# A hybrid decoder block on one core: the modulation's shifts summed by VectorE instead of TensorE

## The chip, the cores and the metric

The kernel runs on one core of one Trainium2 chip. The metric is device microseconds of that core for one execution. The engines are named as the profile names them: PE is TensorE (PEld its weight loads), DVE is VectorE, ACT is ScalarE, POOL is GpSimd, SP is SyncE, which here issues nearly all transfers.

## The reference

One block of width 2048 over a sequence of 256 tokens, in float32. What matters here is the modulation: a conditioning vector `c` of 2048 numbers gives six vectors that shift, scale and gate the two sub-layers.

```python
mod = jax.nn.silu(c) @ w_mod[l] + b_mod[l]            # w_mod: 2048 x (6 * 2048)
sh1, sc1, g1, sh2, sc2, g2 = jnp.split(mod, 6, axis=-1)
h = rms_norm(x, norm1_g[l]) * (1.0 + sc1[:, None]) + sh1[:, None]
proj = h @ w_in[l]                                     # q, k, v, u, gates
...                                                    # attention; S5 scan on u; merge by gates; w_out
x = x + g1[:, None] * (merged @ w_out[l])
h2 = rms_norm(x, norm2_g[l]) * (1.0 + sc2[:, None]) + sh2[:, None]
...                                                    # h2 @ w_up, depthwise conv, gating, w_down
x = x + g2[:, None] * (ffn)
```

Each of the six parts is a product of one row with a 2048 x 2048 matrix: 16 MB of weights that are read once and used once.

## The kernel before

**Weights.** Every matrix comes from HBM in tiles of 128 x 1024 float32 (512 KB), issued by SP one after the other in the order of one list, `plan`. A tile of a dense product is split in two for accuracy: ACT copies it to `whi` (line 186), DVE takes the difference `wlo` (line 191), and PE multiplies both parts. There are five raw tiles in the ring `raw`, two of `whi` and two of `wlo`; the split of a step is issued one step ahead of its matmuls (`split_ahead`). A raw tile is free for the next transfer when its last reader is done. A fourth-stage pool (`post`) adds a second ring of four tiles, `mraw`, for the modulation alone, from the GLU product on.

**Modulation.** Tiles of the modulation are put between the weight steps at a given rate per step (`with_mods`); PE, DVE and ACT meet them in that order.
- The scales and shifts (parts 1, 0, 4, 3) go through `mod_block` (line 443): PE multiplies silu(c), laid out in columns (`cpad`), with the raw tile in four column groups of the array, 128 to 512 columns at a time. A block covers 2 or 4 groups of 128 output channels. When its tiles are through, ACT copies the row sums to SBUF (`rows`, line 463) and `cols_of` (line 475) turns them to columns: PE transposes, one DVE reduction, one addition.
- The gates (parts 2 and 5) go through `gate_block` (line 482): their weights are stored transposed, so that a tile holds half of the inputs of 128 output channels, and one DVE instruction (line 493) multiplies it with silu(c), held on all partitions in `cb`, and sums along the row. `cb` is made by `silu_rows` (line 503) when the `post` pool opens: a transfer of `c` to 128 partitions on POOL's queue (line 505) and one ACT instruction (line 506).

**Stages.** (1) `xT` is loaded, squares are summed for the first norm, and the modulation of the first two channel groups is made. (2) The product with `w_in` runs over the input channels in five chunks (`CHUNKS`, 2, 2, 4, 4, 4 groups of 128): while PE works on a chunk, the scale and then the shift of the next chunk pass by (`mod1`, line 579), and at their end `make_h` modulates the next chunk's `h`. In the last chunk the first quarter of sh2 and sc2 passes (`mod2`, line 1078). The generator `setup` (line 599), which makes the tables of the rotary embedding and of the scan mostly on DVE, runs in the background of these chunks, a piece per 1/0.9 steps; it starts when the scale of the second chunk is there (`place["a1"]`). (3) The rest of the gate products (`gsp`), then `gap` and `pap`: attention and the S5 scan run in the background of these, and the quarters 1 to 3 of sc2 and sh2 pass by at 1.3 tiles a step, but for the last four units (`LATE`), which come after the second norm. (4) `glup`, `ppp` and `outp`, with the tiles of g1 among them, then the second norm. (5) The FFN with the tiles of g2.

**The scan** (`ssm_scan`, line 749) handles eight channel tiles in turn. `prepare` builds the matrices of one tile and ends in the matmuls `bu` (line 815), whose result DVE rotates (lines 852 to 857) and scans (line 862); `leave` multiplies the states out (line 830) and `finish` adds the skip term. Its steps are spread by `yield`, 1.05 to a weight step. `prepare` of the next tile comes before `leave` of the present one, with two buffers of `cpad` and `blocks`, and the tag `s4` has three buffers.

**Queues.** The order of an engine's instructions isn't that of the program text: the build moves an instruction ahead when its inputs are ready and others wait. Within an engine they then run strictly in order, and a waiting one holds up all behind it.

Of the kernel before, what the change touches and what calls it, by code (L numbers as in the profile page):

```python
# [42 lines left out]
def block_kernel(ctx: ExitStack, tc: tile.TileContext, I, out):  # L43
# [54 lines left out]
    LATE = 4  # L98
# [294 lines left out]
    A.activation(cpad[:, :, 0], p0[:, 0:16], AF.Silu)  # L393

    def rsqrt(y, v, t):
        V.tensor_scalar(y.bitcast(I32), v.bitcast(I32), -0.5, 1597463007.0, op0=ALU.mult, op1=ALU.add)
        for _ in range(3):
            V.scalar_tensor_tensor(t, y, -0.5, y, op0=ALU.mult, op1=ALU.mult)
            V.tensor_mul(t, t, v)
            V.scalar_tensor_tensor(y, t, 1.5, y, op0=ALU.add, op1=ALU.mult)  # L400
# [80 lines left out]

    def gate_block(part, k0, nk, cb, dst):

        st = {}
        base = 16 * (part // 5)

        def step(k, half, raw):
            flat = raw.rearrange("p a b -> p (a b)")
            if k == 0 and half == 0:
                st["s"] = sm.tile([128, nk, 2], F32, name="gsum", tag="gsum")  # L490
                V.tensor_copy(st["s"].rearrange("p a b -> p (a b)"), rb[:, 0:2 * nk])
            sums = st["s"]
            V.scalar_tensor_tensor(flat, flat, 1.0, cb[:, 1024 * half:1024 * half + 1024], op0=ALU.mult,  # L493
                                   op1=ALU.mult, accum_out=sums[:, k, half:half + 1])
            if k == nk - 1 and half == 1:
                ks = slice(k0, k0 + nk)
                V.tensor_add(dst[:, ks], sums[:, :, 0], sums[:, :, 1])
                V.tensor_add(dst[:, ks], dst[:, ks], b_mod[:, 16 * part + k0:16 * part + k0 + nk])

        return [[(I["w_g"][base + k0 + k, half], lambda raw, k=k, half=half: step(k, half, raw))]  # L500
                for k in range(nk) for half in range(2)]

    def silu_rows(pool):
        cb = pool.tile([128, 2048], F32, name="cb")
        G.dma_start(cb, I["c"].to_broadcast([128, 2048]))
        A.activation(cb, cb, AF.Silu)
        return cb

# [70 lines left out]
    def mod1(k0, nk):  # L579
# [8 lines left out]

        return mod_block(1, k0, nk, sc, m1_tile) + mod_block(0, k0, nk, sh, bu_tile)

# [5 lines left out]
    def s4(name, shape=(128, 2, 2, 256)):  # L596
        return sp.tile(list(shape), F32, name=name, tag="s4", bufs=3)

    def setup():

        def hold(elem):

            V.tensor_copy(elem, a1[:, place["a1"]:place["a1"] + 1])
# [13 lines left out]
        cs = [take(2, 64) for i in range(2)]  # L617
        bt = s4("bt", (128, 2, 16, 32))
        hold(bt[:, 0, 0, 0:1])
        G.dma_start(bt, I["ssm_b"])  # L620
        yield 1
        while place["a1"] == 0:
# [110 lines left out]
        crb = cre[:, None, :].to_broadcast([128, 16, 32])  # L733
        cib = cim[:, None, :].to_broadcast([128, 16, 32])
        bb = sp.tile([128, 2, 16, 32], F32, name="z_b")
        b2 = s4("b2", (128, 16, 32))
# [12 lines left out]
    def ssm_scan(u):  # L749
# [6 lines left out]
        bpad = sp.tile([128, 2, 2, 4, 2, 16], F32, name="bpad")  # L756
        cpad = [sp.tile([128, 2, 3, 4, 2, 16], F32, name=f"cpad{i}") for i in range(2)]
        blocks = [sp.tile([128, 2, 128], F32, name=f"blocks{i}") for i in range(2)]
        zt = [sp.tile([128, 2, 2, 128], F32, name=f"zt{i}") for i in range(2)]
        dec = sp.tile([128, 2, 4, 64], F32, name="dec")  # L760
        for z in (bpad, *cpad, *blocks, *zt, dec):
            G.memset(z, 0.0)
# [4 lines left out]
        def prepare(ct):  # L767

            tt = slice(4 * ct, 4 * ct + 4)
            cp, kb = cpad[ct % 2], blocks[ct % 2]  # L770
            for g, gs in enumerate(halves):
# [46 lines left out]
        def leave(ct, w):  # L818
            cp, kb = cpad[ct % 2], blocks[ct % 2]
            st["py"] = y = py_tile([128, 2, 128], "py")  # L820
# [21 lines left out]
        for ct in range(8):  # L842
# [39 lines left out]
            yield 1  # L882
            if ct < 7:
                yield from prepare(ct + 1)
            leave(ct, w)
            yield 1
            yield 1
            finish(ct)


# [187 lines left out]
    def mod2(j):  # L1078
        lag = int(j < 3)

        def sc(rows):
            cols_of(rows, 4, 4 * j, 4, a2)
            scale_cols(a2, norm2_g, 4 * j, 4)

        return (mod_block(4, 4 * j, 4, sc, m1_tile, lag)
                + mod_block(3, 4 * j, 4, lambda rows: cols_of(rows, 3, 4 * j, 4, sh2),
                            m1_tile if j < 3 else bu_tile, lag))

# [48 lines left out]
    late = mods[len(mods) - LATE:]  # L1137
    del mods[len(mods) - LATE:]

# [45 lines left out]
    gt = [pair(c + 4, "yg") for c in range(4)]  # L1185
    cb = silu_rows(post)

# [7 lines left out]
    rest, mods[:] = list(mods), []  # L1195
    parts = [m for j in range(4) for m in gate_block(2, 4 * j, 4, cb, g1)]
    while parts or rest:
# [65 lines left out]
    for j in range(4):  # L1263
        mods += gate_block(5, 4 * j, 4, cb, g2)

# [76 lines left out]
def arrange(inputs):  # L1342
# [19 lines left out]
    for n in ("ssm_c_re", "ssm_c_im"):  # L1362
# [6 lines left out]
        "w_m": np.concatenate(w_m),  # L1369
        "w_g": np.concatenate([w_mod[:, 2].T, w_mod[:, 5].T]).reshape(32, 128, 2, 1024).swapaxes(1, 2),  # L1370
        "p0": pack([cols(a["c"]), cols(a["norm1_g"]), cols(a["norm2_g"]), cols(a["b_mod"]), np.eye(128)]),
# [37 lines left out]
```

## Time and profile before

| | |
|---|---|
| time, median of 3 runs (lowest to highest) | 1552.86 us (1548.08 to 1556.23) |
| time of the profiled execution | 1551.37 us |
| its span, first to last instruction | 1549.6 us |
| PE busy | 1491.3 us, 96% |
| PE weight loads busy | 1239.2 us, 80% |
| DVE busy | 1052.7 us, 68% |
| ACT busy | 847.4 us, 55% |
| transfers | 354.54 MB, mean 229 GB/s |
| mean granted TensorE clock | 0.992 of full speed |

The busy time of an engine is the union of its instructions. Matmuls overlap in the pipeline and their ends are modelled, so the cost of a matmul is better read from the distance between the starts of two neighbours than from its own length. A matmul with float32 operands stands in the profile as two records.

### The profile page before, as it was taken

What the parts mean: (1) busy time and instruction counts of PE and PEld (TensorE: products, weight loads), DVE (VectorE), ACT (ScalarE), POOL (GpSimd) and SP (SyncE); (2) the same over time, 40 slices, a digit from 0 to 9 for tenths busy, and PEclk for the clock granted to TensorE, in tenths of its full rate; (3) what the DMA queues carried; (4) which work ended last, traced back from release to release, by engine and by line L of the source; (5) the groups of instructions that cost most, each with busy time, mean ns of one, the idle gap of its engine ahead of it and who ended that gap; (6) DMA issues with size and microseconds to landing.
All of it is one profiled execution on the core that took longest, in us unless ns stands there. A gap on an engine that the chain in (4) does not pass through costs nothing.

```text
span 1549.6 us, 24718 instructions
## 1 busy us (share of the span) xinstructions
PE 1491.3 (96%) x9624; PEld 1239.2 (80%) x9624; DVE 1052.7 (68%) x1778; ACT 847.4 (55%) x1201; POOL 11.3 (1%) x25
## 2 busy tenths in 40 slices
PE   6999989999999999899989999999999999999998
PEld 3656757689886678788869888888888888888887
DVE  2787443786774567799769888887555576666654
ACT  3766656967674543654435555555444455555442
POOL 1000000000000000000000000000000000000000
PEclk9999999999999999999999999999999999999999
DMA  8887777643348776879877777776555555565663
GB/s 308 282 311 279 251 269 255 233 166 121 124 150 284 276 251 209 294 255 345 309 254 241 247 247 257 243 252 207 190 191 190 190 187 190 191 189 189 203 210 111
DMA packets 99252, 354.54 MB, mean 229 GB/s; under 512 B 10976, under 2 KB 13152, under 8 KB 99008
## 3 DMA queue, kind: packets, MB, share of 16 engines
q1 hardware_dynamic: 97808, 348.17, 65.5%
q0 software_dynamic: 1184, 4.66, 0.8%
q8 instruction: 75, 1.23, 0.3%
q14 instruction: 41, 0.34, 0.1%
q10 hardware_dynamic: 144, 0.14, 0.0%
HBM read 350.83 MB, written 2.10 MB: 228 GB/s over the span
## 4 chain that ended last, share of the span: by engine, by line
PE 78%; DVE 8%; DMA 8%; ACT 5%; issue 2%; SPq 0%; ACTq 0%; DVEq 0%; POOLq 0%
PE vp L302 10%; PE dp L302 10%; PE gp L302 10%; PE dp L304 5%; PE vp L304 5%; PE gp L304 5%; DMA raw<-in_w_in_dram 3%; PE outp L302 3%; DVE wlo L191 3%; PE modp L456 3%; PE gap L302 3%; ACT whi L186 2%; PE ppp L302 2%; PE outp L304 2%; PE gap L304 2%
## 5 line engine op out<-in xcount | busy, mean ns | idle before, releaser
L191 DVE TENSOR_TENSOR wlo<-raw,whi 128x1024 fp32r<-128x1024 f32 x464 | 566.8, 1224 | 404.4 <-ACT whi L186 401.9
L186 ACT CAST whi<-raw 128x1024 fp32r<-128x1024 f32 x464 | 486.7, 1050 | 562.3 <-PE dp L302 131.9
L302 PE MATMUL vp<-hl,whi 128*128 128x512 f32 x704 | 247.2, 395 | 0.5 <-DVE gate L1272 0.5
L302 PE MATMUL dp<-g,whi 128*128 128x512 f32 x704 | 244.5, 391 | 0.0
L302 PE MATMUL gp<-hl,whi 128*128 128x512 f32 x640 | 224.5, 395 | 0.0
L304 PE MATMUL dp<-g,wlo 128*128 128x256 f32 x704 | 197.8, 281 | 0.0
L304 PE MATMUL vp<-hl,wlo 128*128 128x256 f32 x704 | 197.4, 280 | 0.0
L304 PE MATMUL gp<-hl,wlo 128*128 128x256 f32 x640 | 179.5, 280 | 0.0
L302 PEld LDWEIGHTS vp<-hl,whi 128*128 128x128 f32 x704 | 132.0, 188 | 31.8 <-issue 0.8
L302 PEld LDWEIGHTS dp<-g,whi 128*128 128x128 f32 x704 | 131.9, 187 | 28.7
L302 PEld LDWEIGHTS gp<-hl,whi 128*128 128x128 f32 x640 | 120.0, 187 | 28.1
L304 PEld LDWEIGHTS dp<-g,wlo 128*128 128x128 f32 x704 | 133.0, 189 | 0.0
L304 PEld LDWEIGHTS vp<-hl,wlo 128*128 128x128 f32 x704 | 133.0, 189 | 0.0
L304 PEld LDWEIGHTS gp<-hl,wlo 128*128 128x128 f32 x640 | 120.9, 189 | 0.0
L302 PE MATMUL gap<-hl,whi 128*128 128x512 f32 x256 | 93.9, 406 | 0.6 <-ACT whi L186 0.5
L302 PE MATMUL outp<-m,whi 128*128 128x512 f32 x256 | 91.2, 400 | 0.2 <-DVE m L1155 0.2
L493 DVE SCALAR_TENSOR_TENSOR mraw<-mraw,cb 128x1024 f32<-128x1024 f32 x64 | 77.8, 1220 | 16.1 <-DMA mraw<-in_w_g_dram 9.2
L456 PE MATMUL modp<-raw,cpad 128*32 128x512 f32 (+1 forms) x544 | 75.2, 561 | 6.0 <-DMA raw<-in_w_m_dram 3.6
L304 PE MATMUL gap<-hl,wlo 128*128 128x256 f32 x256 | 72.9, 285 | 1.1 <-DVE wlo L191 0.9
L304 PE MATMUL outp<-m,wlo 128*128 128x256 f32 x256 | 71.7, 281 | 0.2 <-DVE wlo L191 0.2
L302 PEld LDWEIGHTS gap<-hl,whi 128*128 128x128 f32 x256 | 48.1, 188 | 20.6 <-ACT whi L186 4.2
L302 PEld LDWEIGHTS outp<-m,whi 128*128 128x128 f32 x256 | 48.0, 188 | 14.4 <-issue 2.5
(339 smaller groups left out, 2554.5 us busy)
## 6 DMA issues: line engine op xcount, KB each, us to landing
raw<-in_w_up_dram SPq DMA_DIRECT2D x176, 512.0 KB, 4.3
raw<-in_w_m_dram SPq DMA_DIRECT2D x120, 512.0 KB, 5.2
raw<-in_w_in_dram SPq DMA_DIRECT2D x96, 512.0 KB, 4.8
raw<-in_w_down_dram SPq DMA_DIRECT2D x88, 512.0 KB, 3.5
mraw<-in_w_g_dram SPq DMA_DIRECT2D x64, 512.0 KB, 5.0
raw<-in_w_ga_dram SPq DMA_DIRECT2D x32, 512.0 KB, 3.9
raw<-in_w_out_dram SPq DMA_DIRECT2D x32, 512.0 KB, 5.6
raw<-in_w_attn_br_dram SPq DMA_DIRECT2D x16, 512.0 KB, 4.8
```

The source lines that it names most:

```text
L186: A.copy(hi, loaded[i][0])
L191: V.tensor_sub(lo, loaded[i][0], hi_lo[i][0].bitcast(F32))
L302: follow(PE.matmul(joined(p[m]), hi4[:, k, ms], joined(a), start=u == 0 and k == 0, stop=False, skip_group_check=True))
L304: PE.matmul(p[m][:, 0], lo4[:, k, ms], a[:, 0], start=False, stop=u == kbs - 1 and k == 3, skip_group_check=True)
L456: mm = PE.matmul(st["p"][r0:r0 + 32], cpad[:, k], raw[:, i], start=k < 4, stop=k >= 12, tile_position=(0, r0))
L493: V.scalar_tensor_tensor(flat, flat, 1.0, cb[:, 1024 * half:1024 * half + 1024], op0=ALU.mult, op1=ALU.mult, accum_out=sums[:, k, half:hal ...
```

## The change

It does four things. The shifts sh1 (all but the first two channel groups) and sh2 (its first three quarters) go through `gate_block` instead of `mod_block`; their weights are stored transposed, and their tiles are woven between those of the scales (one unit of the scale, then one or two tiles of the shift). `cb` is made at the start, from one row of `c` that PE spreads over the partitions by a product with ones, and stays; `silu_rows` is gone. The first quarter of g1 passes in the `gap` and `pap` products instead of from the GLU on. To make room for `cb`, the scan gives up a buffer of `s4`, and of `cpad` and `blocks`: `prepare` of the next tile now follows `leave` and `finish`, and the transfer of `ssm_b` (`bt`) moves from the start of `setup` to behind its tables.

```diff
+    cb = const.tile([128, 2048], F32, name="cb")
+    A.dma_start(cb[0:1], I["c"])
+    for i in range(2):
+        p = mm_tile([128, 2, 512], "cb")
+        for j in range(2):
+            PE.matmul(p[:, j], ones[0:1], cb[0:1, 1024 * i + 512 * j:1024 * i + 512 * j + 512], start=True, stop=True)
+        A.activation(cb[:, 1024 * i:1024 * i + 1024], p.rearrange("p a n -> p (a n)"), AF.Silu)
...
-    def gate_block(part, k0, nk, cb, dst):
+    def gate_block(part, k0, nk, dst, done=None):
...
-        base = 16 * (part // 5)
+        base = 16 * (2, 5, 0, 3).index(part)
...
                 V.tensor_add(dst[:, ks], dst[:, ks], b_mod[:, 16 * part + k0:16 * part + k0 + nk])
+                if done is not None:
+                    done()
...
-    def silu_rows(pool):
-        cb = pool.tile([128, 2048], F32, name="cb")
-        G.dma_start(cb, I["c"].to_broadcast([128, 2048]))
-        A.activation(cb, cb, AF.Silu)
-        return cb
+    def woven(units, singles):
+        n = len(singles) // len(units)
+        return [x for i, u in enumerate(units) for x in [u] + singles[n * i:n * i + n]]
...
-        return mod_block(1, k0, nk, sc, m1_tile) + mod_block(0, k0, nk, sh, bu_tile)
+        if k0 == 0:
+            return mod_block(1, k0, nk, sc, m1_tile) + mod_block(0, k0, nk, sh, bu_tile)
+        return woven(mod_block(1, k0, nk, sc, m1_tile), gate_block(0, k0, nk, sh1, lambda: make_h(k0, nk)))
...
-        return sp.tile(list(shape), F32, name=name, tag="s4", bufs=3)
+        return sp.tile(list(shape), F32, name=name, tag="s4", bufs=2)
...
-        bt = s4("bt", (128, 2, 16, 32))          # at the start of setup
-        hold(bt[:, 0, 0, 0:1])
-        G.dma_start(bt, I["ssm_b"])
-        yield 1
...
+        bt = s4("bt", (128, 2, 16, 32))          # behind the tables, ahead of bb
+        hold(bt[:, 0, 0, 0:1])
+        G.dma_start(bt, I["ssm_b"])
...
-        cpad = [sp.tile([128, 2, 3, 4, 2, 16], F32, name=f"cpad{i}") for i in range(2)]
-        blocks = [sp.tile([128, 2, 128], F32, name=f"blocks{i}") for i in range(2)]
+        cp = sp.tile([128, 2, 3, 4, 2, 16], F32, name="cpad")
+        kb = sp.tile([128, 2, 128], F32, name="blocks")
...
+            leave(ct, w)
+            yield 1
+            yield 1
+            finish(ct)
             if ct < 7:
                 yield from prepare(ct + 1)
-            leave(ct, w)
-            yield 1
-            yield 1
-            finish(ct)
...
-        return (mod_block(4, 4 * j, 4, sc, m1_tile, lag)
-                + mod_block(3, 4 * j, 4, lambda rows: cols_of(rows, 3, 4 * j, 4, sh2),
-                            m1_tile if j < 3 else bu_tile, lag))
+        scale = mod_block(4, 4 * j, 4, sc, m1_tile, lag)
+        if j < 3:
+            return woven(scale, gate_block(3, 4 * j, 4, sh2))
+        return scale + mod_block(3, 4 * j, 4, lambda rows: cols_of(rows, 3, 4 * j, 4, sh2), bu_tile, lag)
...
-    del mods[len(mods) - LATE:]
+    mods[len(mods) - LATE:] = gate_block(2, 0, 4, g1)
...
-    cb = silu_rows(post)
...
-    parts = [m for j in range(4) for m in gate_block(2, 4 * j, 4, cb, g1)]
+    parts = [m for j in range(1, 4) for m in gate_block(2, 4 * j, 4, g1)]
...
-        "w_g": np.concatenate([w_mod[:, 2].T, w_mod[:, 5].T]).reshape(32, 128, 2, 1024).swapaxes(1, 2),
+        "w_g": np.concatenate([w_mod[:, i].T for i in (2, 5, 0, 3)]).reshape(64, 128, 2, 1024).swapaxes(1, 2),
```

## Rows read from the trace of the kernel before

**Rows 1.** Busy time by stage: each line is a stretch (us from the span's start), its length, then the busy time of PE, PEld, DVE, ACT and POOL with the number of instructions, the granted TensorE clock, the busy share of the transfer engines and GB/s. The stretches are the work on the first chunk, the second, the third, the fourth and the fifth of `w_in`; `gap` and `pap` from the first modulation tile on; the passage to `glup`; and `glup` to `outp`.
```profile
25.65:59.31 33.66, 32.68 (x202) 23.88 (x203) 20.96 (x70) 18.96 (x23) 0.54 (x1) 0.91 0.82 289
59.31:106.72 47.41, 45.88 (x248) 28.19 (x247) 38.32 (x147) 32.54 (x47) 0.00 (x0) 1.00 0.81 296
106.72:171.34 64.62, 59.72 (x360) 44.05 (x359) 44.52 (x89) 43.49 (x61) 1.60 (x3) 1.00 0.80 282
171.34:239.49 68.15, 62.89 (x368) 46.54 (x367) 27.44 (x38) 40.81 (x58) 0.00 (x0) 1.00 0.72 255
239.49:312.00 72.51, 67.43 (x441) 50.89 (x441) 42.14 (x72) 55.90 (x129) 0.00 (x0) 0.98 0.70 241
456.00:620.00 164.00, 157.05 (x1346) 120.42 (x1346) 101.02 (x155) 74.20 (x102) 0.00 (x0) 1.00 0.71 251
620.00:640.00 20.00, 15.41 (x81) 13.13 (x81) 12.04 (x20) 11.29 (x12) 0.54 (x1) 0.91 0.82 299
640.00:792.00 152.00, 149.67 (x847) 125.71 (x846) 133.39 (x216) 75.51 (x94) 2.85 (x4) 1.00 0.81 294
```

**Rows 2.** PE in order of time: start, length, line, operation, tiles and shapes, number merged in the row. A unit of the modulation among weight steps: one of 128x256 in the first chunk, two records cut off from a unit in the second, a block's transposes, and a unit of 128x512.
```profile
35.43 0.64 PE L456 MATMUL modp<-raw,cpad 128*32 128x256 f32 x8
36.00 0.50 PE L345 MATMUL kp<-whi,hl 128*128 128x512 f32 x1
...
88.28 1.04 PE L456 MATMUL modp<-raw,cpad 128*32 128x512 f32 x2
89.26 0.50 PE L348 MATMUL qp<-wlo,hl 128*128 128x512 f32 x1
...
169.82 0.60 PE L478 MATMUL modt<-p,rows 128*128 128x128 f32 x4
170.17 0.36 PE L268 MATMUL gep<-hl,whi 128*128 128x256 f32 x1
...
180.41 1.06 PE L456 MATMUL modp<-raw,cpad 128*32 128x512 f32 x8
181.40 0.38 PE L268 MATMUL up<-hl,whi 128*128 128x256 f32 x1
```

**Rows 3.** The gate tiles' sums on DVE as a group of instructions: count, busy us and mean ns of one, idle time before them and what ended it.
```profile
L493 DVE SCALAR_TENSOR_TENSOR mraw<-mraw,cb 128x1024 f32<-128x1024 f32 x64 | 77.8, 1220 | 16.1 <-DMA mraw<-in_w_g_dram 9.2 <-ACT cb L506 6.6
```

**Rows 4.** Waits of SP's queue in the five chunks (59 to 312 us): what it waited for, us in total, times, longest.
```profile
SPq L124 <- DVE wlo L191: 76.3, 44, 3.7
SPq L124 <- PE modp L456: 69.2, 23, 5.6
```

**Rows 5.** The passage from `pap` to `glup` in order of time, on ACT, DVE and PE (in brackets the idle time before the row and what ended it); the last line is the transfer of `c`, with its size and the us from issue to landing.
```profile
628.64 1.28 ACT L506 ACT_TABLE_LOAD   x1 [4.63 <-DMA cb<-in_c_dram]
629.93 1.91 ACT L506 ACTIVATE cb<-cb 128x2048 f32<-128x2048 f32 x1
...
631.88 1.23 DVE L493 SCALAR_TENSOR_TENSOR mraw<-mraw,cb 128x1024 f32<-128x1024 f32 x1 [6.61 <-ACT cb L506]
633.03 1.22 DVE L493 SCALAR_TENSOR_TENSOR mraw<-mraw,cb 128x1024 f32<-128x1024 f32 x1
...
620.06 0.39 PE L302 MATMUL glup<-y,whi 128*128 128x512 f32 x1
622.87 0.40 PE L302 MATMUL glup<-y,whi 128*128 128x512 f32 x1
636.11 0.80 PE L302 MATMUL glup<-y,whi 128*128 128x512 f32 x1 [4.59 <-DVE ts L319]
638.83 0.46 PE L302 MATMUL glup<-y,whi 128*128 128x512 f32 x1
...
cb<-in_c_dram POOLq DMA_DIRECT2D x1, 1024.0 KB, 7.7
```

**Rows 6.** The start in order of time, on ACT, PE and SP: the table load behind the first parameters, an early cast of the mask's identity, the first modulation units, and SP's issues for them.
```profile
4.16 1.28 ACT L393 ACT_TABLE_LOAD   x1 [4.16 <-DMA p<-in_p_dram]
6.62 0.28 ACT L730 CAST ident_b<-p 128x128 bf16<-128x128 f32 x1
15.48 1.50 PE L456 MATMUL modp<-raw,cpad 128*32 128x256 f32 x24
4.50 12.49 SPq L124 DMA_DIRECT2D raw<-in_w_m_dram  x8
```

**Rows 7.** Issues of transfers on POOL's queue: number, KB, us from issue to landing.
```profile
bt<-in_ssm_b_dram POOLq DMA_DIRECT2D x1, 512.0 KB, 8.3
z_c<-in_c_re_dram POOLq DMA_DIRECT2D x1, 256.0 KB, 3.0
z_c<-in_c_im_dram POOLq DMA_DIRECT2D x1, 256.0 KB, 3.2
```

**Rows 8.** The scan in order of time: `bu` on PE, then on DVE a split that stands ahead of the rotation while that waits, and one rotation with its sum and scan.
```profile
446.48 2.09 PE L815 MATMUL bu<-u,zt 64*128 64x128 f32 x32
...
593.61 1.22 DVE L191 TENSOR_TENSOR wlo<-raw,whi 128x1024 fp32r<-128x1024 f32 x1
594.75 1.28 DVE L852 TENSOR_TENSOR r<-bu,z_rot 128x512 f32<-128x512 f32 x2
...
450.81 1.28 DVE L854 TENSOR_TENSOR w<-bu,z_rot 128x512 f32<-128x512 f32 x2
452.39 1.29 DVE L857 TENSOR_TENSOR w<-w,r 128x512 f32<-128x512 f32 x2
453.80 1.21 DVE L862 TENSOR_TENSOR_SCAN w<-dec,w 128x512 f32<-128x512 f32 x1
```

More of the change, by code (lines that the diff above doesn't have):

```diff
@@ L756, in ssm_scan @@
         bpad = sp.tile([128, 2, 2, 4, 2, 16], F32, name="bpad")
-        cpad = [sp.tile([128, 2, 3, 4, 2, 16], F32, name=f"cpad{i}") for i in range(2)]
-        blocks = [sp.tile([128, 2, 128], F32, name=f"blocks{i}") for i in range(2)]
+        cp = sp.tile([128, 2, 3, 4, 2, 16], F32, name="cpad")
+        kb = sp.tile([128, 2, 128], F32, name="blocks")
         zt = [sp.tile([128, 2, 2, 128], F32, name=f"zt{i}") for i in range(2)]
         dec = sp.tile([128, 2, 4, 64], F32, name="dec")
-        for z in (bpad, *cpad, *blocks, *zt, dec):
+        for z in (bpad, cp, kb, *zt, dec):
             G.memset(z, 0.0)
@@ L769, in prepare @@
             tt = slice(4 * ct, 4 * ct + 4)
-            cp, kb = cpad[ct % 2], blocks[ct % 2]
             for g, gs in enumerate(halves):
@@ L818, in leave @@
         def leave(ct, w):
-            cp, kb = cpad[ct % 2], blocks[ct % 2]
             st["py"] = y = py_tile([128, 2, 128], "py")
@@ L882, in ssm_scan @@
             yield 1
-            if ct < 7:
-                yield from prepare(ct + 1)
             leave(ct, w)
@@ L888, in ssm_scan @@
             finish(ct)
+            if ct < 7:
+                yield from prepare(ct + 1)
     rq = sm.tile([128, 2, 8], F32, name="rq", tag="rq", bufs=1)
@@ L1263, in block_kernel @@
     for j in range(4):
-        mods += gate_block(5, 4 * j, 4, cb, g2)
+        mods += gate_block(5, 4 * j, 4, g2)
     def conv(t, dst, c0):
```

## The prediction

> **What bounds the kernel now.** I read the page first: PE is busy 96% of the span, DVE 68%, ACT 55%. That is a mean over stages, so the second view is the busy time by stage [rows 1]. From `glup` to `outp` PE works 149.7 of 152 us. In the chunks of `w_in` it does not: 45.9 of 47.4, 59.7 of 64.6, 62.9 of 68.2, 67.4 of 72.5 us. These PE figures are unions of overlapping matmuls and flatter it; the reader should see beside them that transfers run at 241 to 296 GB/s there, and that DVE has 81% in the second chunk but 40% in the fourth. Third, SP's waits [rows 4]: in the chunks it waited 69.2 us, 23 times, for a modulation matmul to give back a raw tile, about as much as the 76.3 us for the split. PE meets a modulation tile late, behind the steps in its queue, and until then the tile keeps one of five places. So the chunks are bound by PE and the ring of raw tiles together. Fourth, the passage to `glup`: PE stands still for 4.59 us [rows 5].
>
> **The change, part by part.**
>
> *Off PE.* Seven shift blocks leave (four of sh1, three of sh2). A block is four units; a unit of 128x512 takes PE from 180.41 to 181.40, 0.99 us, one of 128x256 from 35.43 to 36.00, 0.57 us [rows 2]. Six blocks of the first kind and one of the second: 24 x 0.99 + 4 x 0.57 = 26.0 us. Their transposes: 0.35 us a block (169.82 to 170.17), 7 x 0.35 = 2.5 us. Together 28.5 us. A unit cut up costs more: its first two records alone took 0.98 us (88.28 to 89.26).
>
> *On DVE.* 52 tiles of the shifts (4 + 3 x 8 in the chunks for sh1, 8 there and 16 in `gap`/`pap` for sh2). One costs 1.22 us [rows 3]; two in a row start 1.15 us apart with the read of the sum between (631.88, 633.03) [rows 5]. 52 x 1.15 = 60 us of DVE. Eight tiles of g1 (9 us) move from behind the GLU to `gap`/`pap`.
>
> How much of the 28.5 us reaches the end is decided stage by stage [rows 1].
> - First chunk: PE loses 4 x 0.57 + 0.35 = 2.6 us; DVE goes from 21.0 to 25.6 of 33.7 us. I take -1.5.
> - Second: eight tiles take DVE from 38.3 to 47.5 us, the stage's whole length of 47.4. Nothing can be gained; bounds -5 (PE's 4.3 and the cut-up units) and +5 (DVE's queue full and PE waiting for splits). I take +1.
> - Third: DVE 44.5 + 9.2 = 53.7 of 64.6 us, PE -4.3. The 18 weight and 16 modulation tiles now come one in 1.90 us; 4 us less asks for 1.78 us. I take -3.
> - Fourth: DVE 27.4 + 9.2 of 68.2. PE -4.3, and shift tiles are given back as soon as DVE has summed them, which cuts into SP's 69.2 us. I take -5.
> - Fifth: 42.1 + 9.2 of 72.5, but the scan and the finish of k and q crowd its end. I take -3.
> - `gap`/`pap`: PE -8.6; DVE 101.0 + 24 x 1.15 = 128.6 of 164 us; eight transfers more (4 MB, at the stage's 251 GB/s 16.7 us of traffic, in a stage whose engines are busy 71%). I take -6, between 0 and -12.
>
> Sum of the stages: -17.5 us. Between 640 and 792 us DVE loses 9 us of 133.4, but PE already works 149.7 of 152, so at most 2 us; I take 0.
>
> *The passage to `glup`.* Removed are a transfer of 7.7 us on POOL's queue, a table load of 1.28 and an activation of 1.91 us on ACT; behind these stood the next `whi`, behind `cb` the DVE queue for 6.61 us, and PE for 4.59 us [rows 5]. After that wait PE ran at the lower of its two clock levels for a while (0.91 mean granted clock in 620 to 640 [rows 1]), four pairs of matmuls in 2.72 us (636.11 to 638.83) where eight took 2.81 (620.06 to 622.87), 1.3 us more. With `cb` there, the first sum waits for its own tile only, whose DMAs SP issues in that passage as before. What is late next is `y`, from the scan; I take -5.5, between -2 and -6.
>
> *At the start.* Added on ACT's queue: one transfer of 8 KB and two activations, 1.91 us in all by the same work in [rows 5]; on PE four 512-column products ahead of the squares. A unit of four such in four column groups took 0.99 us; run singly they could take four times that, 4 us. Behind them wait the squares and so the first `modp` at 15.48. That unit also waits for its tiles, which SP issues from 4.50 on [rows 6]. So 0 to +6; I take +2, since ACT is idle until 4.16 us for the parameters and the transfer runs beside that.
>
> *`bt`.* Its transfer goes behind p1, c_re and c_im on POOL's queue, and the four products with it now wait for its landing: 3.0 us by the neighbours of half the size, 8.3 us by itself at the start [rows 7]. If these products stand in DVE's queue ahead of a split, PE has one step of 2.8 us in hand: 0 to +5.5. I take +1.5, nearer the neighbours. A page speaks against this move. The Trainium skill (SBUF — State Buffer, "SBUF: two separate sides" and "A bandwidth-pool intuition that's wrong") has POOL's descriptors written through a port that a vector copy can lock, which holds its transfers up; its example is about 3.1 us in place of 0.62, so by it `bt` would cost 2.5 us more and the sum would be 1533.5, an estimate from that page. The trace does not bear it out: the two neighbours were issued in the third chunk, with DVE at 69%, and landed in 3.0 and 3.2 us.
>
> *The scan.* Its number of steps per tile stays, so its end does. Two `s4` buffers suffice for `w` and `r`, as `prepare` uses none; I cost it at +0.5. What it can cost otherwise is a rival below. ACT loses seven copies of `rows`, the waits of PE's transposes for them go too: -1.
>
> Sum: -17.5 - 5.5 + 2 + 1.5 + 0.5 - 1 = -20. From the profiled execution's 1551.4 us that gives 1531; that execution lies 1.5 us under the median, within the runs' spread.
>
> **The rivals.**
>
> *More comes through.* If PE's 28.5 us all count, with 6 at the passage and 2 to 3 us of waiting for splits in the chunks: 1551 - 37 = 1514. For it: SP's 69.2 us of waits for `modp`, half of which lose their cause. Against: the second chunk's DVE.
>
> *The ring or DVE absorbs it.* If the chunks stay at a tile per 1.9 us whatever PE does, and the eight tiles added to `gap`/`pap` cost what is won there, the passage's 5.5 us remains and the start takes 2: 1548. For it: 282 to 296 GB/s in the second and third chunk already. Against: transfers reached 294 GB/s as a mean over the 152 us from 640, and it is the late return of tiles that holds SP.
>
> *The scan's rotation stalls PE; slower.* Before, `bu` ran some steps ahead of the rotation that reads it. Now no step lies between. PE reaches `bu` behind the present weight step and takes 2.09 us; DVE then rotates (1.28 + 1.28), sums (1.29) and scans (1.21) [rows 8]. If these stand in DVE's queue ahead of the next split (1.2), the split is ready 2.1 + 5.1 + 1.2 = 8.4 us after PE left the step before; PE has one step of 2.8 us to fill that. So 5.6 us a tile, seven tiles: 39 us, and 1531 + 39 = 1570. The deciding point is which stands first. Against it: the queues are not in the order of the text (the cast of line 730 runs at 6.62 us [rows 6]), and at 593.61 a split stands ahead of a rotation that could not start [rows 8].
>
> **How the numbers follow.** The forecast, 1531, has 0.60; its own terms' bounds reach from about 1520 to 1543. More comes through (1514) 0.15; absorbed (1548) 0.14; the scan stalls (1570) 0.11. The range 1511 to 1551 holds the first three but for the tails; the scan's case and some of the absorbed one are left out, near 0.2. A measurement of this kernel tells 0.5%, 7.8 us, from no change: faster means under 1545.1, slower over 1560.6. Faster takes the first two cases and a little of the third, 0.77; same the rest of the third, 0.12; slower the scan, 0.11.
>
> **What would show it.** In the profile after: 352 records of `modp` in place of 576, and 116 sums on DVE in place of 64. The second chunk (59.3 to 106.7 us before) as long as before, with DVE over 95% busy; the fourth shorter by 4 to 6 us. SP's wait for `modp` in the chunks near 35 us. No PE wait over 2 us at the passage to `glup`. The first weight matmul (25.65 us before) at about 27 to 28. It is wrong if `wlo` is what PE waits for right behind each `bu`, if the chunks keep their lengths with PE waiting on `whi`, or if the fourth chunk shrinks no more than the second.

## The result, and the profile after

The kernel after takes 1531.87 us, median of 4 executions (1526.84 to 1536.31), against 1550.47 for the kernel before: ratio 0.989 [0.986, 0.992]. Two more sets, on two chips, gave 1534.17 (0.992 [0.989, 0.995]) and 1530.25 us (0.989 [0.986, 0.993]). So the gain is 13 to 19 us, about 16 in the mean; forecast were 20. The first profiled execution took 1532.5 us, with a span of 1530.6.

SP's waits in the five chunks (59 to 312 us) answer [rows 4]; the sums and the modulation's units as groups (count, busy us and mean ns of one, idle time before them) answer [rows 2, 3].

```profile
SPq L124 <- DVE wlo L191: 89.0, 43, 4.6
SPq L124 <- PE modp L464: 34.3, 12, 5.2
SPq L124 <- DVE raw L501: 22.8, 13, 5.1
```
```profile
L501 DVE SCALAR_TENSOR_TENSOR raw<-raw,cb 128x1024 f32<-128x1024 f32 x60 | 73.0, 1220 | 10.7 <-DMA raw<-in_w_g_dram 9.2 <-PE modp L464 1.3
L501 DVE SCALAR_TENSOR_TENSOR mraw<-mraw,cb 128x1024 f32<-128x1024 f32 x56 | 68.2, 1221 | 12.6 <-DMA mraw<-in_w_g_dram 12.0
...
L464 PE MATMUL modp<-raw,cpad 128*32 128x512 f32 x224 | 34.9, 604 | 1.8 <-DMA raw<-in_w_m_dram 1.8
L464 PE MATMUL modp<-raw,cpad 128*32 128x256 f32 x96 | 12.7, 491 | 0.3 <-DMA raw<-in_w_m_dram 0.2
L464 PE MATMUL modp<-mraw,cpad 128*32 128x512 f32 x32 | 7.8, 651 | 3.1 <-DVE t L407 1.8 <-issue 1.2
```

The wait for `modp` fell from 69.2 to 34.3 us, and 22.8 us of waits for a tile that DVE sums came up in its place, while the wait for splits grew from 76.3 to 89.0. SP still waits most of the time: from the second to the fifth chunk, cut as below, all its waits sum to 207.1 us of 259.6 before and to 204.7 of 251.5 after. So a row that shrinks in this view is not yet a gain; the gain is in the lengths of the stages. There are 60 + 56 = 116 sums and 224 + 96 + 32 = 352 records of `modp`.

Busy time by stage, columns as in [rows 1], first for the first profile of after. From here on a stage is cut where the first matmul of its weight stands: five chunks from `up` to `up` (the last to `gsp`), then `gsp`, then `gap` to the first `ppp` (`gap`, `pap` and `glup`). The stretches of [rows 1] are cut otherwise, so only changes compare with them.

```profile
27.90:64.70 36.80, 36.27 (x203) 27.92 (x204) 22.60 (x49) 21.80 (x28) 0.55 (x1) 0.93 0.76 275
64.70:110.50 45.80, 37.83 (x190) 24.59 (x188) 39.36 (x146) 31.72 (x45) 0.00 (x0) 0.96 0.79 285
110.50:171.40 60.90, 57.39 (x318) 44.71 (x317) 55.72 (x123) 38.30 (x46) 1.81 (x4) 1.00 0.82 294
171.40:238.60 67.20, 59.27 (x347) 45.66 (x346) 44.35 (x79) 44.69 (x65) 0.31 (x1) 1.00 0.80 285
238.60:316.20 77.60, 71.57 (x503) 55.23 (x501) 60.45 (x117) 63.82 (x150) 0.00 (x0) 0.98 0.70 244
316.20:408.30 92.10, 90.34 (x875) 86.27 (x875) 62.69 (x127) 62.54 (x115) 0.00 (x0) 0.98 0.38 127
408.30:634.30 226.00, 211.49 (x1713) 174.25 (x1712) 182.36 (x309) 118.20 (x177) 0.00 (x0) 0.98 0.72 256
```

By these cuts every profile of the study stands in one table (us). "Up to FFN" is the span without the FFN, "ratio" the time against the kernel before on the same chip.

| profile | start | c1 | c2 | c3 | c4 | c5 | gsp | gap to ppp | up to FFN | FFN | ratio |
|---|---|---|---|---|---|---|---|---|---|---|---|
| before | 25.6 | 37.8 | 46.0 | 65.2 | 68.0 | 80.5 | 93.5 | 232.1 | 804.7 | 744.9 | |
| before again (e1) | 26.3 | 37.0 | 45.8 | 63.6 | 66.4 | 79.9 | 93.4 | 234.5 | 801.6 | 744.8 | |
| after | 27.9 | 36.8 | 45.8 | 60.9 | 67.2 | 77.6 | 92.1 | 226.0 | 790.1 | 740.5 | 0.989 |
| after again (e2) | 26.4 | 36.9 | 45.2 | 60.9 | 67.4 | 78.3 | 92.1 | 226.3 | 788.5 | 748.5 | 0.992 |
| after, third (e9) | 26.4 | 36.0 | 47.7 | 60.1 | 66.8 | 77.1 | 90.6 | 223.5 | 784.2 | 744.6 | 0.989 |
| e3 shifts on PE | 25.8 | 37.4 | 47.0 | 66.3 | 64.8 | 82.5 | 91.5 | 225.7 | 799.1 | 744.4 | 0.999 |
| e4 scan edits alone | 24.1 | 38.1 | 48.3 | 65.9 | 64.6 | 84.4 | 91.5 | 233.0 | 804.6 | 742.4 | 1.001 |
| e5 sh1 only | 26.9 | 37.2 | 45.0 | 62.6 | 65.6 | 85.2 | 91.5 | 226.8 | 797.1 | 740.1 | 1.000 |
| e10 sh2 only | 26.2 | 36.3 | 46.6 | 65.4 | 68.0 | 78.6 | 91.4 | 220.0 | 787.7 | 739.5 | 0.992 |
| e6 g1 late | 26.6 | 37.0 | 45.5 | 60.8 | 66.9 | 78.5 | 90.6 | 221.1 | 783.1 | 740.4 | 0.988 |
| e7 silu(c) later | 31.6 | 36.2 | 52.1 | 62.3 | 64.7 | 77.6 | 90.6 | 223.7 | 794.0 | 740.6 | 0.993 |
| e8 early loads | 26.9 | 37.4 | 46.6 | 60.6 | 64.2 | 77.6 | 92.6 | 225.3 | 786.9 | 740.6 | 0.990 |
| e12 units first | 26.5 | 38.5 | 46.8 | 64.9 | 61.9 | 77.8 | 90.4 | 217.4 | 780.0 | 740.4 | 0.990 |

The repeats show what a stage is worth as evidence: up to 2.8 us each, 3 to 6 us for all up to the FFN. A profile is one execution: those of e5, e10 and e12 lie 6 to 10 us under the medians of their runs. The FFN varies by 8 us between executions of the same kernel, which the change does not touch; the last section shows in what. The profiled execution of e11 was a disturbed one (1541.4 us at a granted clock of 0.982, the others 1517.7 to 1529.2 at 0.990 to 0.994) and is left out of its median and of the table.

### The profile page after: what moved, and what is told of

It reads as the page before. It is cut to its first block, busy times and chain, and to the rows that moved or that the text cites. A ratio compares the mean times of both kernels' runs of the same rounds, so it can differ in the third digit from the quotient of the medians.

```text
span 1530.6 us, 24302 instructions
## 1 busy us (share of the span) xinstructions
PE 1469.6 (96%) x9382; PEld 1236.0 (81%) x9382; DVE 1110.3 (73%) x1881; ACT 842.0 (55%) x1193; POOL 9.8 (1%) x22
## 4 chain that ended last, share of the span: by engine, by line
PE 73%; DVE 10%; DMA 9%; ACT 5%; issue 3%; SPq 0%; ACTq 0%; DVEq 0%
PE vp L302 11%; PE dp L302 10%; PE gp L302 10%; PE dp L304 5%; PE vp L304 5%; PE gp L304 5%; DVE wlo L191 4%; PE outp L302 4%; DMA raw<-in_w_in_dram 3%; ACT whi L186 3%; PE gap L302 2%; PE outp L304 2%; PE modp L464 2%; PE ppp L302 2%; DMA raw<-in_w_ga_dram 2%
## 5 line engine op out<-in xcount | busy, mean ns | idle before, releaser
L501 DVE SCALAR_TENSOR_TENSOR raw<-raw,cb 128x1024 f32<-128x1024 f32 x60 | 73.0, 1220 | 10.7 <-DMA raw<-in_w_g_dram 9.2
L501 DVE SCALAR_TENSOR_TENSOR mraw<-mraw,cb 128x1024 f32<-128x1024 f32 x56 | 68.2, 1221 | 12.6 <-DMA mraw<-in_w_g_dram 12.0
```

## The experiments

**e1 and e2: both kernels again.** No edit.

> The kernel before, unchanged, profiled once more. In the first profile PE set off a pair of FFN matmuls (128x512 and 128x256) every 0.3535 us between 840 and 1070 us and every 0.3463 us after 1090, and in the profile after the change every 0.3463 us throughout, which makes 4.4 us of the 19.0 us by which the spans differ. If that pace is a state of the single execution, the FFN (from the first gp matmul to the end, 744.9 us before, 740.5 after) comes out with another mixture here, anywhere from 740 to 753 us. If it belongs to the kernel's layout, 744.9 us again within 0.5. The other stages should repeat within 1 us; that is the measure for all differences by stage.

> The changed kernel, unchanged, with more rounds. Forecast: 20 us under the kernel before, ratio 0.987 to 0.990. If 4.4 us of the first difference were the state of one execution, the ratio by many runs is nearer to 0.991. Stages as in the first profile within 1 us: first chunk 36.8, second 45.9, third 60.9, fourth 67.2 us.

Measured: 1548.19 and 1534.17 us (0.992 [0.989, 0.995]). The stages repeat within 2.4 us, not within the 1 us that was expected. 4.4 us of the difference of the first two profiles lay in the FFN. e1's 744.8 alone is what its second theory, the layout, asked for; but e2's 748.5 against the 740.5 of the same kernel shows that the FFN goes by the execution.

**e3: all shifts on PE again.** The passage and the scan edits stay.

```diff
-        return woven(mod_block(1, k0, nk, sc, m1_tile), gate_block(0, k0, nk, sh1, lambda: make_h(k0, nk)))
+        return mod_block(1, k0, nk, sc, m1_tile) + mod_block(0, k0, nk, sh, bu_tile)
...
-    mods[len(mods) - LATE:] = gate_block(2, 0, 4, g1)
+    del mods[len(mods) - LATE:]
```
(and the same for sh2; all of g1 behind the GLU.)

> The changed kernel with all shifts back on PE and g1's first quarter back behind the GLU; cb from the start, the scan's single buffers and the late bt stay. Theory 1 (the prediction's terms): the 17.5 us of the stages are lost, the passage's 5.5 us stay, start +2, bt and scan +2 less 1: 1 to 2 us under the kernel before. Theory 2 (the passage gave 5 us, the shifts some 10, the late bt cost 4): 0 to +3 us against the kernel before. Rival (the room for cb costs much, and the shifts give all of PE's 28 us): 8 us or more over the kernel before.

Measured: 1544.79 us, ratio 0.999 [0.997, 1.001], or 1.7 us under the kernel before, between 4.8 under and 1.5 over. That is what theory 1 asked for; theory 2's 0 to +3 is not excluded, the rival's 8 or more over is.

**e4: the kernel before with the scan edits and the late `bt` alone.**

```diff
-        return sp.tile(list(shape), F32, name=name, tag="s4", bufs=3)
+        return sp.tile(list(shape), F32, name=name, tag="s4", bufs=2)
...
-            if ct < 7:
-                yield from prepare(ct + 1)
             leave(ct, w)
...
             finish(ct)
+            if ct < 7:
+                yield from prepare(ct + 1)
```
(and the single buffers of `cpad` and `blocks` and the move of `bt`, as in the change.)

> The kernel before with only the scan's edits: two s4 buffers, single cpad and blocks, prepare behind finish, bt behind the tables. Prediction's terms: +0.5 for the scan and +1.5 for bt, +2 us. Theory 2: bt and c_re are waited for by DVE, some 5 us in one place, of which 3 to 5 reach the end: +3 to +5 us. The rival of the prediction (the rotation stands ahead of the next split): 5.6 us in each of seven tiles, +39 us, with waits of PE for wlo behind each bu.

Measured: 1548.51 us, 1.001 [0.999, 1.003]. Scan edits and late `bt` cost 2 us with an interval of -1 to +5, so the scan does not stall PE, which would have cost 39; the prediction's +2 and theory 2's +3 to +5 are not told apart. Against e4, e3 has in addition silu(c) made at the start: `gap` to `ppp` falls from 233.0 to 225.7 us. Only 4.0 of these 7.3 us lie in `glup` (26.2 to 22.2), the rest in `gap` and `pap`, within what repeats differ by. Against the kernel before, `glup` falls from 28.5 and 30.3 (e1) to e3's 22.2, and `gap` and `pap` keep their length. Either way it is about 7 us, the second time with the scan edits in it. The wait itself was shorter in e4 already, where the transfer of `c` still stood but landed in 5.0 us instead of 7.7. What PE waits for at the passage (total, times, longest), before, in e4, and after:

```profile
PE glup L302 <- DVE ts L319: 4.6, 1, 4.6
```
```profile
PE glup L302 <- DVE ts L319: 1.9, 1, 1.9
```
```profile
PE glup L302 <- DVE ts L319: 0.6, 1, 0.6
```

**e5, e10, e6: one norm's shifts at a time.** With e3 these make a square: all four have the passage and the scan edits and all of g1 behind the GLU. e5 has only sh1 on DVE, e10 only sh2, e6 both. They ran on three chips, so each is compared with the kernel before on its own. e6 is therefore also the kernel after with eight g1 tiles taken out of `gap`/`pap`; its edit is

```diff
-    mods[len(mods) - LATE:] = gate_block(2, 0, 4, g1)
+    del mods[len(mods) - LATE:]
...
-    parts = [m for j in range(1, 4) for m in gate_block(2, 4 * j, 4, g1)]
+    parts = [m for j in range(4) for m in gate_block(2, 4 * j, 4, g1)]
```
and e5 and e10 add one half of e3's edit.

> Only the first norm's shifts (chunks two to four) are summed by VectorE; sh2 is back on TensorE and all of g1 stands behind the GLU tiles. If the shifts' gain comes in the chunks c2 to c4 and c5 by TensorE's relief, and gap/pap gained only from the passage, this run lies 1 to 4 us above the kernel after: c1 to c5 stay within 2 us of the kernel after in sum (about 335 us against 339 to 343 with the shifts on TensorE), gap to glup stays at 226, the output stage is 2 to 3 us longer (16 g1 half-tiles more behind GLU). If instead the second norm's shifts carried half of the gain, gap to glup is 5 us or more longer than 226 and the time lies 6 us or more above the kernel after.

> The fourth corner of a square with the runs of both shifts on TensorE, of the first norm's shifts alone on VectorE, and of both (all four with g1 behind GLU): only the second norm's shifts are on VectorE. If the two parts simply add, chunks one to four keep the length that they have with all shifts on TensorE (215 us; 210 with the first norm's on VectorE), the fifth chunk falls to 76 to 79 us (82 to 85 with the second norm's shifts on TensorE), and gap to glup is 220 to 222 us instead of 226 to 227. If the fifth chunk's and the gap's gain need fewer units left over from the chunks before, the fifth chunk stays at 82 us or more and gap to glup at 225 or more.

> The kernel after, but with the first quarter of g1 behind the GLU tiles as before, so that gap and pap hold 8 tiles fewer. If the 8 tiles (4.2 MB at the ring's pace, 8 sums on VectorE) used up what TensorE saved there, gap to glup falls from 226 to 218 to 222 us and the output stage grows by 2 to 4 us: the time lies 1 to 5 us below the kernel after. If gap and pap are set by the splits and transfers of their weight tiles, whatever the modulation does, gap to glup stays within 2 us of 226 and the output stage grows by 2 to 4 us: the time is 1 to 4 us above.

Measured: e5 1546.30 us, 1.000 [0.998, 1.003]; e10 1535.39, 0.992 [0.989, 0.994]; e6 1526.34, 0.988 [0.984, 0.992]. Up to the FFN, against e3's 799.1: sh1 alone -2.0, sh2 alone -11.4, both -16.0 us. The times say the same, against e3's (in us of 1547: +2, -11, -17). So sh2 carries the gain. sh1's part, -2.0 alone and -4.6 beside sh2, lies within what repeats differ by (3 to 6 us), and so does the difference between -16.0 and the sum of the two alone, -13.4; e10's first theory, that the parts add, gets its stages (216.3 us for chunks one to four, 78.6 and 220.0). e5's first alternative, a kernel 1 to 4 us above after, is refuted: by the ratios it stands 13 to 17 us above. Its condition for the other, `gap` to `ppp` at 231 or more, was not met either (226.8), because that number compared a stage with eight g1 tiles against one without.

SP's waits show where sh2 sits. First e5, then e6, in the fifth chunk:

```profile
SPq L124 <- DVE wlo L191: 30.4, 16, 3.4
SPq L124 <- DMA raw<-in_w_in_dram: 18.6, 7, 3.6
SPq L124 <- PE modp L464: 8.6, 3, 4.9
```
```profile
SPq L124 <- DVE wlo L191: 29.2, 15, 4.0
...
SPq L124 <- DMA raw<-in_w_in_dram: 5.9, 5, 2.3
```

and from `gap` to `ppp`, e5 and then e6:

```profile
SPq L124 <- DVE wlo L191: 88.2, 36, 6.9
SPq L124 <- PE modp L464: 48.3, 15, 6.1
```
```profile
SPq L124 <- DVE wlo L191: 91.1, 41, 6.9
SPq L124 <- DVE raw L501: 14.2, 8, 3.1
SPq L124 <- PE modp L464: 13.7, 5, 5.3
```

With sh2 on PE, SP stood 48.3 us behind units there; with sh2 on DVE 13.7 us behind units and 14.2 behind sums, and the stage is 5.7 us shorter (226.8 to 221.1), the fifth chunk 6.7. But SP's waits for other DVE work grew there from 31.8 to 52.0 us, and all its waits fell only from 189.3 to 187.3. In the fifth chunk the wait for units hardly changed (8.6 to 7.1); the wait for landings fell (18.6 to 5.9). So these rows show who holds the tiles, and not by which way the 5.7 us came about: PE's relief and the tiles' earlier return come with the same edit, and no run separates them. The eight g1 tiles then cost it back: 221.1 (e6) against 226.0, 226.3 and 223.5 (after), 4.2 us in the mean. That is e6's first theory; only the 2 to 4 us that it allowed for the output stage did not come (`ppp` and output took 156.1 us against 155.1 to 155.9).

In e5, what sh1 gave in the second and third chunk (-5.7 against e3) was in part lost again in the fourth and fifth (+3.5).

**e7: silu(c) on all partitions made behind the first norm's sums.** The block of `cb` stands ahead of `setup()` instead of behind the first activation; nothing is taken out.

> The kernel after, but with silu(c) on all partitions made behind the first norm's statistics (row, products and activations moved, none taken out). If the four products at the start cost what the first weight matmul shows (27.9 against 25.6 to 26.3 us), the first weight matmul is back at 25.5 to 26.5 us and the time 0 to 2 us below the kernel after. If the start is set by the raw tiles' transfers and the difference was that of executions, the first weight matmul stays at 26.4 to 28 us and the time within 1.5 us of the kernel after.

Measured: 1535.27 us, 0.993 [0.991, 0.996]; the first weight matmul at 31.6. Both theories missed. PE at the start, first after, then e7:

```profile
4.05 7.16 PE L400 MATMUL cb<-cb,ones 1*128 1x512 f32 x8 [4.05 <-DMA cb<-in_c_dram]
11.42 2.23 PE L464 MATMUL modp<-raw,cpad 128*32 128x256 f32 x16 [0.20 <-DMA raw<-in_w_m_dram]
...
27.88 0.58 PE L268 MATMUL up<-hl,whi 128*128 128x256 f32 x1 [1.00 <-ACT hl L579]
```
```profile
4.15 2.04 PE L1029 MATMUL cb<-cb,ones 1*128 1x512 f32 x2 [4.15 <-DMA cb<-in_c_dram]
6.12 1.33 PE L533 MATMUL sqs<-sq,ones 128*32 128x256 f32 x8
7.38 2.07 PE L1029 MATMUL cb<-cb,ones 1*128 1x512 f32 x2
...
13.48 2.07 PE L1029 MATMUL cb<-cb,ones 1*128 1x512 f32 x2
...
17.35 2.07 PE L1029 MATMUL cb<-cb,ones 1*128 1x512 f32 x2
...
31.57 0.39 PE L268 MATMUL up<-hl,whi 128*128 128x256 f32 x1 [1.00 <-ACT hl L571]
```

In after the products run from 4.05 to 11.2 us, ahead of the first unit, whose tile came just then (0.20 us of wait): they fill the time until it. In e7 half of them fall behind that point, between squares and units that the norm waits for. Of the two places the one at the very front is the cheaper. Why e7's second chunk is 4 to 7 us longer as well (52.1) stays open.

**e8: the scan's rows loaded early.** `ssm_b` goes straight into `z_b` and is scaled in place; with c_re, c_im and p1 it is issued ahead of the tables.

```diff
+        bb = sp.tile([128, 2, 16, 32], F32, name="z_b")
...
+        G.dma_start(bb, I["ssm_b"])
+        cc = sp.tile([128, 2, 32, 16], F32, name="z_c")
+        for dst, n in ((p1, "p1"), (cc[:, 0], "c_re"), (cc[:, 1], "c_im")):
...
+            G.dma_start(dst, I[n])
         V.tensor_copy(pos, pos_i)
...
-        bt = s4("bt", (128, 2, 16, 32))
...
-        G.dma_start(bt, I["ssm_b"])
...
```

> The kernel after, but with the transfers of the scan's input and output rows (ssm_b straight into its place, c_re, c_im, p1) issued ahead of the tables, no product more or less. If VectorE's 5 us of waits for those rows is what held the fourth and fifth chunk (67.2 and 77.6 us in the kernel after, 64.6 to 64.8 for the fourth with the scan edits and TensorE's shifts), VectorE's waits for c_re and ssm_b are gone and the fourth chunk is 3 to 5 us shorter; the time is 3 to 5 us below the kernel after. If the ring and TensorE set the chunk's end and VectorE had room, the waits are gone and the chunks c3 to c5 stay within 1.5 us in sum of 205 to 206 us: the time within 1.5 us of the kernel after.

Measured: 1531.39 us, 0.990 [0.987, 0.994]. DVE's waits for these rows are gone, the fourth chunk is 2.9 us shorter than after's mean of 67.1, and chunks three to five 3.0 (202.4 against 205.4). By stage the first theory comes out at its lower end, by one profile; the time doesn't resolve 3 us.

**e9: the kernel after a third time,** on the chip of e10 to e12.

> The kernel after once more, on the chip of the next three, so that their times stand beside it. Its time against the kernel before should lie where the first two sets put it: ratio 0.988 to 0.994, 9 to 18 us below. By stages: gap to glup 225 to 227 us, chunks one to five 288 to 290 us, the FFN at 740 or 748 us by the pace that this execution gets.

Measured: 1530.25 us, 0.989 [0.986, 0.993]; two stages fell just outside (`gap` to `ppp` 223.5, the chunks 287.7), and the FFN, at 744.6, was neither of the two that were expected.

**e11: e6 and e8 together.**

> The two edits that helped, together: the scan's rows loaded ahead of the tables, and the first quarter of g1 behind the GLU tiles. If they add, the fourth chunk is 64 to 65 us (67.2 in the kernel after), gap to glup 220 to 222 us (226), and the time is 6 to 10 us below the kernel after on this chip, about 1523 us. If the one takes the other's gain (the g1 tiles then stand nearer to the end of the scan), it is 2 to 5 us below.

Measured: 1524.47 us, 0.985 [0.982, 0.988]; the kernel after on the same chip had 1530.25. The lowest time of the study, 5.8 us under after by the medians, between the two theories' ranges, and the intervals overlap. It beats the kernel before clearly, the kernel after probably; whether the two edits add is not settled.

**e12: e11 with the second chunk's four units ahead of its eight rows,** so that the scales on which the scan's setup waits are there earlier.

```diff
+        if k0 == 4:
+            return mod_block(1, k0, nk, sc, m1_tile) + gate_block(0, k0, nk, sh1, lambda: make_h(k0, nk))
```

> The same as the run of the two edits together, but in the second chunk the four scale units stand ahead of the eight transposed rows instead of between them, so that the first norm's second block of scales, on which the scan's setup waits, is there about six tiles earlier. If the late setup is what makes the third and fourth chunk's VectorE work pile up, VectorE's busy time moves from the fourth and third chunk (27 to 44 and 45 to 56 us in the kernel after) into the second, and chunks three and four are 2 to 4 us shorter in sum. If the ring sets these chunks' ends, VectorE's work moves the same way and the chunks' sum stays within 1.5 us of the run before this one (about 125 us).

Measured: 1531.75 us, 0.990 [0.987, 0.993]. DVE's time moved as both theories say: the second chunk has 42.2 us of it against 38.1 in e8, the fourth 36.9 against 41.6. The fourth chunk fell by 2.3 us and the third grew by 4.3, so their sum did not fall (126.8 against e8's 124.8); it lies outside both theories' ranges. Moving this part of the setup forward doesn't shorten these chunks; which of ring and PE sets them was not separated. The profile, at 1522.2 us, is the fastest of the six executions, so its short `gap` to `ppp` (217.4) is not read as a gain.

## Why the prediction was right

The direction held, and the size in the main (13 to 19 us against 20). That the passage and the shifts carry the gain is shown by the runs that undo them: the passage with the scan edits is worth some 7 us, the shifts 16.0 (e3 to e6), and the eight g1 tiles take 4.2 back. Which part of the shifts' gain is PE's relief and which the tiles' earlier return stays open. In the single terms there is luck: the fourth chunk gave 4.9 us less than forecast, `gap`, `pap` and the passage 3.5 less, while `gsp`, the start and a cost taken for `bt` and the scan came out 4 us better. One of the prediction's own signs of being wrong did show: the fourth chunk shrank no more than the second (both unchanged within repeats). Mean of three profiles of after minus mean of two of before, beside the forecast:

| step | forecast | measured | |
|---|---|---|---|
| first chunk | -1.5 | -0.8 | within repeats |
| second chunk | +1 | +0.3 | length right, its reason wrong |
| third chunk | -3 | -3.8 | |
| fourth chunk | -5 | -0.1 | **mis-sized** |
| fifth chunk | -3 | -2.5 | |
| `gsp` | 0 | -1.9 | from the scan edits: 91.5 in e4 already |
| `gap`/`pap` and passage | -6 - 5.5 | -8.0 | **passage 7, shifts and g1 tiles about 0** |
| `ppp` to the FFN | 0 | +0.2 | |
| start | +2 | +0.9 | |
| FFN | 0 | -0.3 | |
| `bt`, scan, ACT | +1 | in the rows above | |
| sum | -20 | -16.0 | times: -13 to -19 |

*Second chunk.* It kept its length, but DVE is busy 39.4 of 45.8 us, 86% and not over 95%. The eight sums stand in this chunk as forecast (9.7 us, and eight more in the third). What left it is the scan's setup, for the reason that follows: its own instructions on DVE fell from 18.2 to 6.1 us here and rose from 12.6 to 23.4 in the third chunk, whose DVE is busy 55.7 us.

*Fourth chunk: the step that failed.* PE's units left it (62.9 us busy in [rows 1], 59.3 now), as forecast. The term that failed is the return of tiles, "given back as soon as DVE has summed them": SP's waits in this chunk, before (174.56 to 242.56 us) and after (171.4 to 238.6), are

```profile
SPq L124 <- DVE wlo L191: 23.2, 14, 3.1
SPq L124 <- PE modp L456: 14.1, 4, 5.4
SPq L124 <- DMA raw<-in_w_in_dram: 13.2, 5, 3.6
```
```profile
SPq L124 <- DVE wlo L191: 31.9, 17, 4.6
SPq L124 <- DVE raw L501: 11.9, 4, 5.1
SPq L124 <- PE modp L464: 8.0, 2, 4.3
```

The 6.1 us that SP no longer stood behind units, and 12.0 that it no longer stood behind landings (1.2 us are left), came back as 11.9 behind sums and 8.7 more behind splits: here DVE is late. One reason is a move that the prediction did not follow. The setup waits at three places for a block of scales; woven among the rows, such a block ends later. What stands behind these blocks ran at 45.1, 85.4 and 141.6 us before and runs at 57.3, 109.0 and 169.2 now. The setup's transfers were issued at 142 to 143 us before; after, POOL (start, us, what it issued) has them 27 us later:

```profile
170.12 0.54 POOL L735 DMA_DIRECT2D z_c<-in_c_re_dram  x1
...
171.18 0.54 POOL L743 DMA_DIRECT2D bt<-in_ssm_b_dram  x1
```

and DVE, in order of time, waits for them at the head of the fourth chunk:

```profile
170.70 1.22 DVE L191 TENSOR_TENSOR wlo<-raw,whi 128x1024 fp32r<-128x1024 f32 x1 [0.29 <-ACT whi L186]
175.97 0.29 DVE L794 TENSOR_TENSOR q<-z_c,z_lam 128x128 f32<-128x128 f32 x1 [4.05 <-DMA z_c<-in_c_re_dram]
176.18 1.22 DVE L501 SCALAR_TENSOR_TENSOR raw<-raw,cb 128x1024 f32<-128x1024 f32 x1
...
177.33 1.22 DVE L191 TENSOR_TENSOR wlo<-raw,whi 128x1024 fp32r<-128x1024 f32 x1
179.46 0.69 DVE L749 TENSOR_TENSOR z_b<-bt,scr 128x512 f32<-128x512 f32 x1 [0.91 <-DMA bt<-in_ssm_b_dram]
```

DVE stood 4.05 us for c_re and 0.91 for `bt`, with a sum and a split behind each. The lateness follows the weaving of sh1: DVE waits 3.7 to 4.9 us for c_re in e5, e2 and e9, and 0.2 to 0.4 in e3, e4 and e10, where sh1 is on PE. e8 takes these waits away, and its chunk is 2.9 us shorter. DVE's work in the chunk rose from 27.4 [rows 1] to 44.4 us, where 36.6 were forecast. That is not the whole cause. With sh1 on PE and the same scan edits the fourth chunk takes 64.8, 64.6 and 68.0 us (e3, e4, e10); against two of these e8's 64.2 is hardly less, so even with the waits gone little of PE's relief is seen here. How the rest of the forecast's 5 us is lost stays open.

*`bt`.* It landed in 8.2 us and c_re in 5.8, nearer the far end of the bounds (8.3) than the neighbours' 3.0 that the prediction took. The 2.9 us that e8 takes back lie in the range of 0 to 5.5, but the larger wait is the one for c_re, which the prediction had not priced. The transfers, with their size and the us from issue to landing:

```profile
bt<-in_ssm_b_dram POOLq DMA_DIRECT2D x1, 512.0 KB, 8.2
z_c<-in_c_re_dram POOLq DMA_DIRECT2D x1, 256.0 KB, 5.8
```

The prediction weighed a rule of the Trainium skill (SBUF — State Buffer, "SBUF: two separate sides"), by which a busy vector copy would hold POOL's transfers up. The landing of c_re did grow by about 3 us, but DVE ran nothing in the last 4.05 of its 5.8 us, so for most of that time no vector instruction can have held it. Other transfers are a candidate that no run isolates: 304 GB/s ran beside it, against 220 while it landed in 3.0 us before.

*`gap`/`pap` and the passage.* Together 8.0 of 11.5. The passage gave rather more than forecast (some 7 us, as shown under e4; PE's wait 4.59 us before, 0.56 after), the shifts 4.6 (e3 to e6), and the eight g1 tiles took 4.2 back (e6 to after). The prediction named these tiles and left them inside -6; they should have been a term of their own.

*Start.* The first weight matmul came at 26.4 to 27.9 us, forecast 27 to 28. The four products took 7.16 us, beyond the bound of 4 that was worked out from a unit; it cost only 1 us, presumably because the first unit waited for its tile until 11.4 anyhow and the squares, which ran from 6.3 us on before, now run between the units.

*The rivals.* *More comes through* fails, on the fourth chunk and on the g1 tiles above all; with both eased, in e11, the gain is about 23 us, not 37. *Absorbed* fails: with all shifts on PE (e3) the kernel is 11 to 15 us slower than after. *The scan's rotation stalls PE* is refuted by e4, and by PE's waits of 420 to 610 us in after:

```profile
PE gap L304 <- DVE wlo L191: 4.5, 6, 1.9
PE pap L272 <- DVE wlo L191: 2.8, 5, 1.1
...
PE bu L823 <- ACT zt L804: 1.1, 2, 0.7
```

The rival needed 5.6 us behind each of seven `bu`; all waits for `wlo` there are 7.3 us, the longest 1.9.

## What to carry to other kernels

When work moves from the engine that returns buffers late to one that returns them soon, expect the wait of the queue that issues the loads to change its owner rather than to vanish: take the gain from the length of the stage in a run that undoes the move. Charge each tile added to a stage as a term of its own. When a list is interleaved, look for what starts only when its last piece is done: here 27 us of lateness in a setup, which no sum over the whole kernel shows. And undo each half of a change singly: of two halves of 28 and 24 tiles the smaller gave 11.4 us alone, the larger 2.0, which repeats do not tell from nothing.

## What was not expected of the hardware

PE has two paces in the same code at the same granted clock. In the FFN a pair of matmuls (128x512 and 128x256) starts every 0.346 us in some long stretches and every 0.353 us in others, and which it is changes from execution to execution of one kernel. The stretch 840 to 1060 us by engine (columns as in [rows 1]), for after and its repeat e2:

```profile
840.00:1060.00 220.00, 220.00 (x1271) 192.38 (x1270) 181.76 (x284) 123.86 (x159) 0.00 (x0) 1.00 0.73 248
```
```profile
840.00:1060.00 220.00, 220.00 (x1247) 190.88 (x1246) 178.96 (x278) 122.25 (x157) 0.00 (x0) 1.00 0.72 245
```

PE is full in both and the clock column is 1.00 in both, but 1271 matmuls ran against 1247. The pace makes about 4 us of the FFN: e9, at the slow pace in this stretch as e2 is, takes 744.6 us against 740.5. The other 4 us of e2's 748.5 lie ahead of the stretch, for the most part in a wait of PE with a lower granted clock behind it (0.91 from 820 to 840 us):

```profile
827.70 0.77 PE L302 MATMUL vp<-hl,whi 128*128 128x512 f32 x1 [2.43 <-DVE gate L1279]
```

The cause of the two paces stays open. For the reader it means that two single profiles can differ by 8 us with no change at all.
